# A walk of its own for each of 21 weight blocks: strided weights, regrouped columns, split matmuls

## The chip, the cores and the metric

The kernel runs on one core of a Trainium2 chip. The metric is the device time of one execution in microseconds, the median over the runs of the kernel. A second view is one profiled execution, whose span is counted from its first to its last instruction.

## The reference

One decoder block over 256 tokens of width 2048, in float32: an attention branch and a state-space branch, merged by gates, and then a feed-forward part. What the change touches is the up-projection of that last part:

```python
D_MODEL = 2048
SEQ = 256
D_FF = 5632
...
        x = x + merged @ w_out[i]
        h = rms_norm(x, ffn_norm_g[i])
        val, gate = jnp.split(h @ w_up[i], 2, axis=-1)
        gate = causal_depthwise_conv(gate, conv_w[i], conv_b[i])
        x = x + (val * jax.nn.gelu(gate, approximate=False)) @ w_down[i]
    return rms_norm(x, final_norm_g)
```

`w_up` is 2048 x 11264, by far the largest of the weights. The kernel holds the activations transposed, with the features on the 128 partitions and the 256 tokens along the columns.

## The kernel before

**Units and blocks.** Every weight matrix is cut into units of 128 partitions x 1024 columns (512 KB). A unit holds eight 128 x 128 weight tiles. 416 units are walked in one fixed order, `units`. The projections q, kv, u, ga, gs, the attention and state-space outputs A and S, glu and o come first. Then come the 22 up-projection blocks `up0` to `up21` of eight units each (block j yields 256 value and 256 gate features), and four down-projection blocks `dn0` to `dn3`.

**Precision.** The kernel keeps nearly full float32 precision with matmuls of a reduced format, `float32r`. ScalarE rounds a unit `raw` to `whi` (a CAST), and VectorE computes the rest, `wlo = raw - whi`. The activations are split likewise, once, into `Ah` and `Al`, which lie side by side in `x2g`: for each of the 16 groups of 128 features there are 256 columns of `Ah` and then 256 of `Al`. A product is then `whi*Ah + whi*Al + wlo*Ah`.

**Two ways to multiply.** In the first stages and in `up0` each weight tile takes three matmuls of 256 columns (`whi` with `Ah`, `whi` with `Al`, `wlo` with `Ah`), all into one accumulator. From `up1` on, and in `dn0` to `dn2`, the accumulator is a whole 512-column bank of PSUM for each tile. There one matmul of 512 columns takes `whi` over `Ah` and `Al` together, and one of 256 columns takes `wlo` over `Ah` into the first half. These two matmuls are called a **pair** below. A block has 16 feature groups x 4 tiles = 64 pairs. The two halves of the bank are added when the block is read out (`whole`, in `ev_up`). Each matmul instruction loads its own 128 x 128 weight tile first, also where it is the same tile as before.

**What sets the order.** The order is written out: the loop over the units multiplies unit i, and then `prep(i + LOOK)` rounds the unit five places ahead and issues the load of the unit nine places ahead (`load(i + 4)` inside `prep`). There are four buffers of `raw` and five each of `whi` and `wlo`. The program keeps clocks of its own, `clk_v`, `clk_a` and `clk_pe`, only to decide where the attention and state-space work is put in; that work is over before `up1`.

**Where the buffers lie.** A buffer of `whi` or `wlo` is a tile of 1032 floats, of which 1024 are used, so that the next buffer starts 4128 bytes on.

**The line numbers.** All engine calls go through the helper `Counted`, so almost every row of the profile has its one line, L132. Rows are told apart by the tile names.

Of the kernel before, what the change touches and what calls it, by code (L numbers as in the profile page):

```python
# [8 lines left out]
F32 = mybir.dt.float32  # L9
F32R = mybir.dt.float32r  # L10
I32 = mybir.dt.int32
AF = mybir.ActivationFunctionType
ALU = mybir.AluOpType
AX = mybir.AxisListType

P = 128
T = 256
# [6 lines left out]
LOOK = 5  # L24
# [33 lines left out]
def _units():  # L58
    def block(name, K, m):
        kw = 1024 // (m * P)  # L60
        return [(name, K, m, k0, kw) for k0 in range(0, K, kw)]

    def pair(x, y):
        return [u for both in zip(x, y) for u in both]

    out = pair(block("q0", NK, 4), block("u", NK, 4)) + block("kv", NK, 2) + block("q1", NK, 4)
    for n, K in (("ga", NK), ("gs", NK), ("A", 8)):
        for c in range(3 if n == "A" else 4):
            out += block(f"{n}{c}", K, 4)
    g0 = block("glu0", 4, 4)  # L70
    out += g0[:1] + block("A3x", 8, 2) + block("A3y", 8, 2) + g0[1:] + block("glu1", 4, 4) + pair(block("S0", 4, 4), block("S1", 4, 4))
    for n, c, K in [("S", 2, 4), ("S", 3, 4)] + [("o", c, NK) for c in range(4)]:
        out += block(f"{n}{c}", K, 4)
    for c in range(22):
        out += block(f"up{c}", NK, 4)
    for c in range(4):
        out += block(f"dn{c}", NFF, 4)
    return out


class Tally:
# [56 lines left out]
def hybrid_block_kernel(  # L138
# [14 lines left out]
    V, S = Counted(nc.vector, clk_v, dve_ns), Counted(nc.scalar, clk_a, act_ns)  # L153
    PE = Counted(nc.tensor, clk_pe, pe_ns)

    base = ctx.enter_context(tc.tile_pool(name="base", bufs=1))
    strm = ctx.enter_context(tc.tile_pool(name="strm", bufs=1))
# [6 lines left out]
    def close_pool(cm):  # L164
        cm.__exit__(None, None, None)
# [17 lines left out]
    A = base.tile([P, NK, 2, T], F32R, tag="A", name="xg")  # L183
# [21 lines left out]
    units = _units()  # L205
# [14 lines left out]
    def load(u, parts=1):  # L220
        if u >= NU:
            return
        raws[u] = strm.tile([P, 1024], F32, tag="raw", name=f"raw{u}", bufs=4)
        arrive[u] = fetch(1456.0, clk_v.ns if u > 3 else 0.0)
        n = 1024 // parts
        for i in range(parts):
            nc.sync.dma_start(raws[u][:, i * n : (i + 1) * n], wst[u, :, i * n : (i + 1) * n])

    prepped = {}

    def prep(i, parts=1):
        if i >= NU:
            return
        raw = raws.pop(i)
        clk_a.ns = max(clk_a.ns, clk_pe.ns if i >= LOOK else 0.0, arrive.pop(i))
        hi = strm.tile([P, 1032], F32R, tag="whi", name=f"whi{i}", bufs=LOOK)[:, 0:1024]
        lo = strm.tile([P, 1032], F32R, tag="wlo", name=f"wlo{i}", bufs=LOOK)[:, 0:1024]
        n = 1024 // parts
        for j in range(parts):
            sl = slice(j * n, (j + 1) * n)  # L240
            S.copy(hi[:, sl], raw[:, sl])
            clk_v.ns = max(clk_v.ns, clk_a.ns + 130.0)
            V.tensor_tensor(lo[:, sl], raw[:, sl], hi[:, sl].bitcast(F32), op=ALU.subtract)
        prepped[i] = (hi, lo, clk_v.ns)
        if i >= 4:
            load(i + 4)
# [51 lines left out]
    st = {}  # L298
# [514 lines left out]
    def finish(key):  # L813
        while key not in st:
            assert any([advance(e, True) for e in list(gens)])
# [146 lines left out]
    def begin(name):  # L962
        if name == "glu0":
            finish("su1")
        elif name == "o0":
            st["X"] = base.tile([P, NK, T], F32, tag="X", name="xres")
            nc.gpsimd.dma_start(st["X"], xT)
            A2 = base.tile([P, NK, 2, T], F32R, tag="A", name="x2g")
            st["A"], st["Ah"], st["Al"] = A2, A2[:, :, 0], A2[:, :, 1]
            A2 = mid.tile([P, 2, 4, T], F32, tag="tA", name="sqA")  # L970
            st["sq"], st["sq2"] = A2[:, 0], A2[:, 1]
        elif name == "dn0":
            A3 = base.tile([P, 2, NK, T], F32, tag="A", name="xo_sq")
            st["xo"] = A3[:, 0]
            st["sq"], st["sq2"] = A3[:, 1, 0:4], A3[:, 1, 4:8]
# [27 lines left out]
    def drain():  # L1003
        while held:
            after(clk_v, clk_pe)
            after(clk_a, clk_pe)
            evac(*held.pop(0))

    for i, (name, K, m, k0, kw) in enumerate(units):
        if k0 == 0:  # L1010
            begin(name)
            if name == "q1":
                finish("rs")
                drain()
            elif name == "A0":
                finish("attn")
            elif name == "o0":
                finish("m3")
            elif name == "up1":
                finish("rs2")  # L1020
                assert not gens and not aux
            if name[:2] == "dn" or name[:2] == "up" and name != "up0":
                if name == "up1":
                    close_pool(ax_cm)
                    wide_cm, pool = open_pool("wide_b", space=PSUM, side="right")
                    wide = [pool]
                elif name == "up2":
                    close_pool(acc_cm)
                    wide_cm2, pool = open_pool("wide_a", space=PSUM, side="left")
                    wide.append(pool)  # L1030
                nf += 1
                accs[name] = wide[nf % 2 - 1].tile([P, 4, 512], F32, tag="wide", name=f"acc_{name}")
            elif name == "kv":
                accs[name] = bank("pq", m, T)
            elif name[:2] == "A3":
                accs[name] = bank("at" if name == "A3x" else "pq", m, T)
            else:
                accs[name] = accp.tile([P, m, T], F32, tag="acc", name=f"acc_{name}")
        if name == "glu0" and k0 == 2:
            finish("su3")  # L1040
        acc = accs[name]
        mh, ml = mover(name)
        hi, lo, ready = prepped.pop(i)
        clk_pe.ns = max(clk_pe.ns, ready)
        hi = hi.rearrange("p (k m c) -> p k m c", k=kw, m=m)
        lo = lo.rearrange("p (k m c) -> p k m c", k=kw, m=m)
        if name == "dn3" and i >= NU - TAIL:
            tail.append((k0, hi, lo))
            prep(i + LOOK)
            continue  # L1050
        double = acc.shape[2] == 512 and name != "dn3"
        for kk in range(kw if double else 0):
            k = k0 + kk
            both = (st["A"] if name[0] == "u" else st["H"])[:, k].rearrange("p s t -> p (s t)")
            for c in range(m):
                PE.matmul(acc[:, c], hi[:, kk, c], both, start=k == 0, stop=False, skip_group_check=True)
                PE.matmul(acc[:, c, 0:T], lo[:, kk, c], mh[:, k], start=False, stop=k == K - 1, skip_group_check=True)
        for kk in range(0 if double else kw):
            k = k0 + kk
            for c in range(m):  # L1060
                o = acc[:, c, 0:T]
                first = k == 0 and (c % 2 == 0 or name == "dn3")
                last = k == K - 1
                PE.matmul(o, hi[:, kk, c], mh[:, k], start=first, stop=False, skip_group_check=True)
                PE.matmul(o, hi[:, kk, c], ml[:, k], start=False, stop=False, skip_group_check=True)
                PE.matmul(o, lo[:, kk, c], mh[:, k], start=False, stop=last, skip_group_check=True)
                run_aux()
            if kk == 0:
                fill()
        if i + LOOK < NK:  # L1070
            xg(i + LOOK, "ag")
        if i in (1, 3):
            load_x(i + 11, 2)
        if i == 3:
            nc.sync.dma_start(pr[:, 48:], par[:, 48:])
            nc.sync.dma_start(ident, cst[:, 0:P])
        if i == 6:
            nc.sync.dma_start(cs, cst[:, P:512])
            nc.sync.dma_start(cT, ssmc)
            st["consts"] = True  # L1080
        for e in gens:
            e[1] -= 1
        fill()
        if k0 + kw == K:
            held.append((name, acc))
        prep(i + LOOK)
        if "rs" in st:
            drain()
        if k0 + kw == K and name == "o3":
            spawn(g_norm2())  # L1090
        if k0 + kw == K and name == "dn2":
            spawn(g_pre(), 2)
# [17 lines left out]
    for n in range(4):  # L1110
        o = (aux, acc)[n % 2][:, n // 2 * 2, 0:T]
        for k0, hi, lo in tail:
            for kk in range(2):
                k = k0 + kk
# [20 lines left out]
    for c0, c1 in zip(cuts, cuts[1:]):  # L1135
        o = xo[:, c0:c1]
# [102 lines left out]
```

## Time and profile before

| what | value |
|---|---|
| median of 2 runs | 1249.06 us (1249.02 to 1249.1) |
| the profiled execution, its time | 1248.1 us |
| the profiled execution, its span | 1246.3 us |
| granted TensorE clock over the span | 0.996 |
| PE (matmuls) busy | 99% of the span, 8476 matmuls |
| PEld (weight loads) busy | 90%, 8476 loads |
| VectorE busy | 69% |
| ScalarE busy | 50% |
| DMA | 228.29 MB, mean 183 GB/s |

PE is the matrix engine and PEld its weight loads, which overlap the matmuls. Matmuls are pipelined, so that one shown with 280 ns can start 118 ns after the one ahead of it: the cost of a matmul in a stream is read from the distance of the starts, not from its duration. The chain of work that ended last is the list of the profile that says what the end of the kernel waited for, back to its first instruction. Shapes read as partitions x elements.

### The profile page before, as it was taken

Reading aid. Unit: us, or ns where it says so; the run is one execution under the profiler, and the core shown is the slowest. Engines: PE = TensorE matmul, PEld = TensorE weight load, DVE = VectorE, ACT = ScalarE, POOL = GpSimd, SP = SyncE. Lnnn points to the kernel's source line nnn. Section 1 sums busy time; section 2 is a strip of 40 time slices with the busy share of each in tenths; the row PEclk is TensorE's granted clock in tenths of the full one; section 3 lists DMA queues with packets and bytes.
Section 4 is the critical chain, followed back from the end, with each engine's and each line's share of the span. In section 5 each row is a group of like instructions: output and inputs, shape, how many; then the busy total and the mean of one; then the engine's idle time right before and its main releaser. Section 6 shows DMA issues by size and latency. Waiting matters only on the chain.

```text
span 1246.3 us, 20901 instructions
## 1 busy us (share of the span) xinstructions
PE 1232.6 (99%) x8476; PEld 1127.8 (90%) x8476; DVE 857.5 (69%) x1220; ACT 619.8 (50%) x865; POOL 10.4 (1%) x24
## 2 busy tenths in 40 slices
PE   9999999999999999999999999999999999999996
PEld 9999999899999999988888888888888888888996
DVE  6987888889978656666767666666676654454543
ACT  7667455454435545544555445455455444343531
POOL 0000000000000000000000000000000000000000
PEclk9999999999999999999999999999999999999998
DMA  8655444444445665555564655646546564656451
GB/s 313 208 196 185 154 151 159 144 160 155 155 169 184 240 197 175 178 192 171 179 219 144 218 186 172 216 153 212 194 151 219 171 221 160 218 162 218 156 201 68
DMA packets 64896, 228.29 MB, mean 183 GB/s; under 512 B 7648, under 2 KB 9056, under 8 KB 64672
## 3 DMA queue, kind: packets, MB, share of 16 engines
q1 hardware_dynamic: 63648, 223.55, 54.1%
q0 software_dynamic: 1152, 3.41, 0.9%
q8 instruction: 66, 1.08, 0.4%
q14 instruction: 30, 0.25, 0.1%
HBM read 224.31 MB, written 2.10 MB: 182 GB/s over the span
## 4 chain that ended last, share of the span: by engine, by line
PE 97%; DVE 1%; DMA 0%; ACT 0%; SPq 0%; issue 0%; DVEq 0%
PE acc_up L132 40%; PE acc_dn L132 19%; PE acc_ga L132 8%; PE acc_gs L132 7%; PE acc_o L132 7%; PE acc_q L132 3%; PE acc_A L132 3%; PE pq L132 2%; PE at L132 2%; PE acc_S L132 2%; PE acc_u L132 1%; PE yp L132 1%; PE acc_glu L132 1%; PE aux L132 1%; DVE xo_sq L132 0%; DMA x_in<-in_xT_dram 0%
## 5 line engine op out<-in xcount | busy, mean ns | idle before, releaser
L132 DVE TENSOR_TENSOR wlo<-raw,whi 128x1024 fp32r<-128x1024 f32 (+2 forms) x421 | 501.5, 1210 | 272.4 <-ACT whi L132 268.4
L132 ACT CAST whi<-raw 128x1024 fp32r<-128x1024 f32 (+2 forms) x421 | 428.9, 1037 | 416.0 <-PE acc_dn L132 110.4
L132 PE MATMUL acc_up<-x2g,whi 128*128 128x512 f32 (+1 forms) x1472 | 494.1, 385 | 0.0
L132 PE MATMUL acc_up<-x2g,wlo 128*128 128x256 f32 x1408 | 395.1, 281 | 0.0
L132 PEld LDWEIGHTS acc_up<-x2g,whi 128*128 128x128 f32 x1472 | 272.1, 188 | 59.0
L132 PEld LDWEIGHTS acc_up<-x2g,wlo 128*128 128x128 f32 x1408 | 265.3, 188 | 0.0
L132 PE MATMUL acc_dn<-H,whi 128*128 128x512 f32 (+1 forms) x856 | 242.7, 351 | 0.0
L132 PE MATMUL acc_dn<-H,wlo 128*128 128x256 f32 x692 | 194.0, 280 | 0.0
L132 PEld LDWEIGHTS acc_dn<-H,whi 128*128 128x128 f32 x856 | 149.2, 188 | 22.8
L132 PEld LDWEIGHTS acc_dn<-H,wlo 128*128 128x128 f32 x692 | 130.7, 189 | 0.0
L132 PE MATMUL acc_ga<-xg,whi 128*128 128x256 f32 x512 | 93.4, 284 | 0.0
L132 PE MATMUL acc_gs<-xg,whi 128*128 128x256 f32 x512 | 93.2, 284 | 0.0
L132 PEld LDWEIGHTS acc_ga<-xg,whi 128*128 128x128 f32 x512 | 78.4, 188 | 2.8 <-issue 2.0
L132 PEld LDWEIGHTS acc_gs<-xg,whi 128*128 128x128 f32 x512 | 78.3, 188 | 2.6 <-issue 1.7
L132 PE MATMUL acc_ga<-xg,wlo 128*128 128x256 f32 x256 | 72.0, 281 | 0.0
L132 PE MATMUL acc_gs<-xg,wlo 128*128 128x256 f32 x256 | 72.0, 281 | 0.0
L132 PE MATMUL acc_o<-mh,whi 128*128 128x256 f32 x256 | 71.8, 281 | 0.0
L132 PE MATMUL acc_o<-ml,whi 128*128 128x256 f32 x256 | 71.7, 280 | 0.0
L132 PE MATMUL acc_o<-mh,wlo 128*128 128x256 f32 x256 | 71.6, 280 | 0.0
L132 ACT ACTIVATE cy<-cy 128x512 f32<-128x512 f32 x22 | 13.9, 632 | 69.9 <-DVE cy L132 69.9
L132 PEld LDWEIGHTS acc_o<-mh,wlo 128*128 128x128 f32 x256 | 48.2, 188 | 0.0
L132 PEld LDWEIGHTS acc_ga<-xg,wlo 128*128 128x128 f32 x256 | 48.2, 188 | 0.0
(212 smaller groups left out, 1407.8 us busy)
## 6 DMA issues: line engine op xcount, KB each, us to landing
raw<-in_wst_dram SPq DMA_DIRECT2D x415, 512.0 KB, 4.3
xres<-in_xT_dram POOLq DMA_DIRECT2D x1, 2048.0 KB, 10.1
x_in<-in_xT_dram SPq DMA_DIRECT2D x7, 256.0 KB, 5.8
out_dram<-xo_sq SPq DMA_DIRECT2D x7, 256.0 KB, 2.4
br<-in_ssmb_dram POOLq DMA_DIRECT2D x3, 256.0 KB, 4.9
raw<-in_wst_dram SPq DMA_DIRECT2D x2, 256.0 KB, 2.9
cT<-in_ssmc_dram SPq DMA_DIRECT2D x1, 512.0 KB, 5.1
us<-ul POOLq DMA_DIRECT2D x16, 32.0 KB, 2.6
```

The lines of the kernel that those rows point to most:

```text
L132: return fn(*a, **k)
```

## The change

The change touches the blocks `up1` to `up21` and the place of all the weight buffers. Each of the 21 blocks gets a triple `(ws, g, one)` of the table `FORMS`, in order:

- `ws` is the **weight step**. For `ws` 1 a tile's 128 columns are neighbours, as before. For 2, 4 or 8, that many tiles are interleaved, so that a tile's next column is 2, 4 or 8 floats (8, 16 or 32 bytes) on. The CAST and the subtraction write `whi` and `wlo` in that order (`woven`), the subtraction reads `whi` in that order, and the matmul loads its weights with that step (`wt`).
- `g` is the **column walk**. For 0 the moving columns go in order, as before. For g of 4 to 32 the matmul takes every second group of g columns first and then the groups between; the output columns go the same way (`mv`). For -1 both go backwards.
- `one` is 1 for one matmul of 512 columns with `whi`, as before, and 0 for two of 256, each with its own weight load.

The first block's triple `(1, 0, 1)` is the walk of before. Seven blocks have step 2 (`up8` to `up14`), four step 4 (`up15` to `up18`) and one step 8 (`up21`). Ten blocks are split (`one` = 0): `up5` to `up7`, `up11` to `up14`, `up17`, `up18` and `up20`. Twelve are walked in groups: g = 4 in `up2`, 8 in `up12`, 16 in six and 32 in four. `up19` and `up20` go backwards. The results are the same sums, in the same places of PSUM.

The buffers of all 416 units become tiles of 1040 floats, and the used part starts 0, 4, 8, 12 or 12 floats into its tile, by the unit's number modulo 5.

```diff
+FORMS = [(1, 0, 1), (1, 4, 1), (1, 16, 1), (1, 32, 1), (1, 0, 0), (1, 16, 0), (1, 32, 0),
+         (2, 0, 1), (2, 16, 1), (2, 32, 1), (2, 0, 0), (2, 8, 0), (2, 16, 0), (2, 32, 0),
+         (4, 0, 1), (4, 16, 1), (4, 0, 0), (4, 16, 0), (1, -1, 1), (1, -1, 0), (8, 0, 1)]
...
+    def woven(i, ap, rows=False):
+        name = units[i][0]
+        s = FORMS[int(name[2:]) - 1][0] if name[:2] == "up" and name != "up0" else 1
+        if s == 1:
+            return ap
+        if rows:
+            return ap.rearrange("p (a s c) -> p a s c", s=s, c=P)
+        return ap.rearrange("p (a c s) -> p a s c", c=P, s=s)
...
-        hi = strm.tile([P, 1032], F32R, tag="whi", name=f"whi{i}", bufs=LOOK)[:, 0:1024]
-        lo = strm.tile([P, 1032], F32R, tag="wlo", name=f"wlo{i}", bufs=LOOK)[:, 0:1024]
+        o = (0, 4, 8, 12, 12)[i % LOOK]
+        hi = strm.tile([P, 1040], F32R, tag="whi", name=f"whi{i}", bufs=LOOK)[:, o : o + 1024]
+        o = (0, 4, 8, 12, 12)[i % LOOK]
+        lo = strm.tile([P, 1040], F32R, tag="wlo", name=f"wlo{i}", bufs=LOOK)[:, o : o + 1024]
...
-            S.copy(hi[:, sl], raw[:, sl])
+            S.copy(woven(i, hi[:, sl]), woven(i, raw[:, sl], True))
...
-            V.tensor_tensor(lo[:, sl], raw[:, sl], hi[:, sl].bitcast(F32), op=ALU.subtract)
+            V.tensor_tensor(woven(i, lo[:, sl]), woven(i, raw[:, sl], True), woven(i, hi[:, sl].bitcast(F32)),
+                            op=ALU.subtract)
...
-        for kk in range(kw if double else 0):
+        form = FORMS[int(name[2:]) - 1] if double and name[:2] == "up" else None
+        if form:
+            ws, g, one = form
+
+            def mv(ap):
+                return ap[:, ::-1] if g < 0 else ap.rearrange("p (n t g) -> p t n g", t=2, g=g) if g else ap
+
+            def wt(w, b):
+                w = w.rearrange("p k m c -> p (k m c)")
+                if ws < 2:
+                    return w[:, P * b : P * b + P]
+                return w.rearrange("p (a c s) -> p a c s", c=P, s=ws)[:, b // ws, :, b % ws]
+
+            for kk in range(kw):
+                k = k0 + kk
+                xb = st["A"][:, k].rearrange("p s t -> p (s t)")
+                for c in range(m):
+                    for o in (slice(0, 2 * T),) if one else (slice(0, T), slice(T, 2 * T)):
+                        PE.matmul(mv(acc[:, c, o]), wt(hi, kk * m + c), mv(xb[:, o]), start=k == 0 and o.start == 0,
+                                  stop=False, skip_group_check=True)
+                    PE.matmul(mv(acc[:, c, 0:T]), wt(lo, kk * m + c), mv(xb[:, 0:T]), start=False, stop=k == K - 1,
+                              skip_group_check=True)
+        for kk in range(kw if double and not form else 0):
```

No instruction changes its place on any engine. What changes is the form of matmuls, CASTs and subtractions, and that a split block has 64 matmuls more. On PE, the start of block `up2`, form `(1, 4, 1)`; before:

```order
L132 MATMUL acc_up_6542<-x2g,whi_6424 128x512
L132 MATMUL acc_up_6542<-x2g,wlo_6425 128x256
L132 MATMUL acc_up_6542<-x2g,whi_6424 128x512
L132 MATMUL acc_up_6542<-x2g,wlo_6425 128x256
L132 MATMUL acc_up_6542<-x2g,whi_6424 128x512
```

And now (the helper's line is L139 after the change; the last number is g, and the one ahead of it the groups of each of the two rounds):

```order
L139 MATMUL acc_up_6542<-x2g,whi_6424 128x2x64x4
L139 MATMUL acc_up_6542<-x2g,wlo_6425 128x2x32x4
L139 MATMUL acc_up_6542<-x2g,whi_6424 128x2x64x4
L139 MATMUL acc_up_6542<-x2g,wlo_6425 128x2x32x4
L139 MATMUL acc_up_6542<-x2g,whi_6424 128x2x64x4
```

The same pairs stand in the same places; only their columns are taken in two rounds. On PE, the start of block `up17`, form `(4, 0, 0)`; before:

```order
L132 MATMUL acc_up_9497<-x2g,whi_9383 128x512
L132 MATMUL acc_up_9497<-x2g,wlo_9384 128x256
L132 MATMUL acc_up_9497<-x2g,whi_9383 128x512
L132 MATMUL acc_up_9497<-x2g,wlo_9384 128x256
L132 MATMUL acc_up_9497<-x2g,whi_9383 128x512
```

And now:

```order
L139 MATMUL acc_up_9945<-x2g,whi_9831 128x256 x2
L139 MATMUL acc_up_9945<-x2g,wlo_9832 128x256
L139 MATMUL acc_up_9945<-x2g,whi_9831 128x256 x2
L139 MATMUL acc_up_9945<-x2g,wlo_9832 128x256
L139 MATMUL acc_up_9945<-x2g,whi_9831 128x256 x2
```

Each matmul of 512 columns has become two of 256, so that a pair is now three matmuls with three weight loads; the step of the weights does not show in these rows.

## The prediction

> **What bounds the kernel now.** I read the chain of work that ended last first, for what the end of the kernel waits for. The page has it by engine and line:
>
> ```profile
> PE 97%; DVE 1%; DMA 0%; ACT 0%; SPq 0%; issue 0%; DVEq 0%
> ```
>
> So only what happens to the matmul stream counts at first order. The same chain in order of time, for the stages o, `up` and `dn` (start us, us, what, count):
>
> ```profile
> 400.59 90.36 PE acc_o L132 x768
> ...
> 506.35 479.28 PE acc_up L132 x2757
> 985.63 238.13 PE acc_dn L132 x1512
> ```
>
> These rows give the price of a matmul in an unbroken stream. Stage o has matmuls of 256 columns alone: 90.36 / 768 = 117.7 ns each. The `up` row holds 69 more of that kind, from the end of `up0` (8.12 us), and then 21 x 128 = 2688 matmuls, that is 21 blocks or 1344 pairs, in 471.16 us. So a block is **22.44 us** and a pair **350.6 ns**, of which the 512-column matmul takes 350.6 - 117.7 = 232.9.
>
> Next I read the timeline inside a block, matmuls and weight loads together (start us, us):
>
> ```profile
> 700.14 0.40 PE L132 MATMUL acc_up<-x2g,whi 128*128 128x512 f32 x1
> 700.15 0.19 PEld L132 LDWEIGHTS acc_up<-x2g,wlo 128*128 128x128 f32 x1
> 700.38 0.28 PE L132 MATMUL acc_up<-x2g,wlo 128*128 128x256 f32 x1
> 700.38 0.19 PEld L132 LDWEIGHTS acc_up<-x2g,whi 128*128 128x128 f32 x1
> 700.49 0.39 PE L132 MATMUL acc_up<-x2g,whi 128*128 128x512 f32 x1
> ```
>
> A load starts when the matmul ahead of its own starts, and not earlier. One load is under way per matmul. The load from 700.38 ends at 700.57, and its matmul starts at 700.49, 0.08 us before that end. So a load of length L keeps two matmul starts at least L - 80 ns apart: 188 - 80 = 108 ns today, just inside the 117.7 of 256 columns. **The weight load is the second bound of the stream**, covered with 10 ns to spare by 256 columns, and with 125 by 512.
>
> What a load costs by its columns (last column: mean ns):
>
> ```profile
> L132 PEld LDWEIGHTS acc_up<-x2g,wlo 128*128 128x128 f32 x1408 | 265.3, 188 | 0.0
> ...
> L132 PEld LDWEIGHTS yp<-xa,cT 128*32 128x32 f32 x64 | 5.7, 109 | 5.5
> ...
> L132 PEld LDWEIGHTS at<-pt,vtok 128*64 128x64 f32 x64 | 3.9, 136 | 2.2
> ```
>
> From 64 to 128 columns it grows by 52 ns, from 32 to 64 by 27: 0.82 ns per column, so 105 of the 188 ns go with the columns.
>
> **The change part by part.** *Split matmuls.* Where loads stay as they are, three matmuls of 117.7 take the place of 350.6: 353.1, or +2.5 x 64 = 0.16 us a block. Eight of the ten split blocks have steps 1 or 2: 1.3 us.
>
> *Weight step.* No load with a step is in the trace. The nearest rows are VectorE's reads when it fills the table E by doubling. The rows with 64 elements read runs of 2 floats out of every 512 bytes, those with 32 single floats, those with 128 and 256 runs of 4 and 8:
>
> ```profile
> L132 DVE TENSOR_TENSOR ea<-E 128x256 f32<-128x256 f32 x1 | 0.4, 425 | 0.0
> ...
> L132 DVE TENSOR_TENSOR ea<-E 128x128 f32<-128x128 f32 x1 | 0.3, 294 | 0.0
> ...
> L132 DVE TENSOR_TENSOR ea<-E 128x64 f32<-128x64 f32 x1 | 0.2, 235 | 0.0
> L132 DVE TENSOR_TENSOR ea<-E 128x32 f32<-128x32 f32 x1 | 0.2, 233 | 0.0
> ```
>
> The slope from 128 to 256 is 1.02 ns per element. On that line 64 elements should take 229 (measured 235) and 32 should take 196 (measured 233). Runs of two are nearly free, and a single float per place costs 37 / 32 = 1.2 ns more, about double. The same in another row, 16 single floats against 16 neighbours:
>
> ```profile
> L132 DVE TENSOR_TENSOR sp<-E x3: 190/192/194, 108.4 to 108.9; 128x16 f32<-128x16 f32 x3
> ...
> L132 DVE TENSOR_TENSOR sp<-sp 128x16 f32<-128x16 f32 x7 | 0.9, 171 | 0.0
> ```
>
> 21 / 16 = 1.3 ns more. I carry this over to the loads: step 2 free, steps 4 and 8 double the 105 ns. The Trainium skill, SBUF — State Buffer, section Specifications (TRN2), gives lines of 16 bytes that need at least two hits each for full bandwidth; two floats a line remain with step 2, one with 4 or 8. For VectorE the rows agree; no row here shows it for a weight load, and the sums stand on the rows alone.
>
> A doubled load is 293 ns. Starts are then 293 - 80 = 213 ns apart, or 117.7 + 105 = 223 if the load sets the 117.7 already; I take 218. A whole pair (`up15`, `up16`, `up21`): the 512-column matmul still covers its load, so 232.9 + 218 = 451, +100.3 x 64 = 6.4 us a block, **19.3 us**. A split pair (`up17`, `up18`): 3 x 218 = 654, +303.4 x 64 = 19.4 us a block, **38.8 us**. The bounds: nothing, where a load reads each float at one price whatever the step; a gain is excluded, since 117.7 is then set by the columns. And 1.3 x 128 = 168 ns more a load, by the dearest row: starts 276 to 286 apart, say 281; whole pairs +211 (13.5 us x 3), split ones +492 (31.5 us x 2), 103.5 us together. I take the doubling, as it is the row with the most elements.
>
> *CAST and subtraction.* They are off the chain while they keep up. In one block (us, busy per engine):
>
> ```profile
> 520.00:542.43 22.43, 22.43 (x131) 19.61 (x130) 12.58 (x14) 11.40 (x14) 0.00 (x0) 1.00 0.58 187
> ```
>
> The columns after the length are PE, PEld, VectorE and ScalarE. Steps 4 and 8 make eight subtractions of a block read single floats: 8 x 1024 x 1.2 = 9.8 us, VectorE 22.4. That fills a block of today, but such a block lasts 28.9 us or more in the sum; if its loads stay short, the lead of five units (11 us and more) takes up what is over. ScalarE has 11.40 and no strided row; doubled writes would add 8 x 1.05 = 8.4, also covered. Both cost nothing.
>
> *Column walk.* Groups of 4 to 32 keep runs of at least four floats, which cost VectorE nothing in the rows above. I take 0 here and for backwards; it is rival D.
>
> *Buffer places.* They reach all 416 units. Three units in a row, each from its first matmul to the next one's:
>
> ```profile
> 632.13:634.97 2.84, 2.84 (x19) 1.00 0.27 107
> 634.97:637.74 2.77, 2.77 (x19) 1.00 0.00 0
> 637.74:640.55 2.81, 2.81 (x19) 1.00 0.00 0
> ```
>
> The same matmuls take 2.84 and 2.77 us at a granted clock of 1.00. The second and third units pass without a byte of DMA (0.00), so it isn't the loads; the buffers differ. Against the mean, 22.44 / 8 = 2.805, that is ±0.035 us: ±14.6 us over 416 units if all fell on one side. I take 0, since the old places were mixed and the new ones are too.
>
> **The sum:** 1.3 + 19.3 + 38.8 = +59.4 us. The profiled execution took 1248.1 (span 1246.3, the rest before and behind it), so 1307.5. The median of the runs is 1.0 above that execution: **1308 us**.
>
> **The rivals.** *B, the loads don't care for the step.* The order of the weights then changes nothing on PE, ten splits cost 1.6 us, and it ends at 1251, within 2%. For it: loads run on a path of their own, and VectorE's price need not hold there. It decides up to a load of 198 ns (117.7 + 80), beyond which 256 columns no longer cover it; the doubled load has 293. The Trainium skill, TensorE: Matmul & The Clock Gate, section LDWEIGHTS (loading the stationary operand), has a load's time go by its columns alone, P / 1.2 ns: by that rule it is B, 1251. The three rows above agree, but all have dense weights.
>
> *C, step 2 costs too,* half as much as 4: starts 168 ns apart in seven blocks, 3.2 us in each of three whole ones and 9.8 in each of four split ones, some 48 on top: 1357. Against it: 235 measured where 229 is on the line.
>
> *D, the walk breaks the stream.* If each jump between groups cost 1.1 ns, about what a single place costs VectorE, a pair has 768 / g jumps: 13.5 us for `up2`, 6.8 for `up12`, 3.4 in four blocks with g = 16 (two more hide behind slow loads) and 1.7 in four with 32. That is 41 us on top: 1349; backwards blocks would come under it too. For it: no matmul of the trace has such columns. The Trainium skill, PSUM — Partial Sum Buffer, section Specifications (TRN2), says that any non-contiguous access slows matmuls significantly; its lines there are of 8 bytes, which runs of four floats fill. No run here shows it yet.
>
> *E, faster.* The new places and walks win the whole spread of 2.84 to 2.77 for all units: 416 x 0.07 = 29 us, 1220, and the loads cost nothing. Against it: it needs B, and a mixed set of places as good as the best.
>
> **How the numbers follow.** The forecast has 0.56, B 0.18, D 0.13, C 0.08, E 0.05. A kernel 2% off, 25 us, can be told from no change. The forecast's own range is 1291 (placement, the 213) to 1354 (the dear load). The range of 8 in 10 takes in B with most of its placement, D and half of C: 1240 to 1360. It leaves out E and the outer ends of the others, below 2 in 10. Slower by over 2%: forecast, C and D, less a little for partly covered loads, 0.75. Within: B and that little, 0.20. Faster: E, 0.05.
>
> **What would show it.** Block lengths in the chain or the windows: 22.4 us for `up1`, the same for `up2` to `up4` and `up8` to `up10`, 22.6 for split blocks of steps 1 and 2, 28.9 for `up15`, `up16` and `up21`, 41.9 for `up17` and `up18`. Weight loads of 293 ns in those five blocks and 188 in all others. Subtractions of 2.4 us there, and no PE idle time ahead of these blocks. Stage o at 117.7 ns a matmul within 1%. It is wrong if loads of step 4 stay at 188 (B), if those of step 2 grow (C), if `up2` is longer than `up4` (D), or if block `up1`, whose walk is the old one, moves by more than 1% (placement).

## The result: 1324.87 us, 6% slower

The changed kernel takes 1324.87 us (median of 2 runs, 1324.72 to 1325.02) against 1249.06 before: a ratio of 1.0607, with a 95% interval of 1.0561 to 1.0653. The prediction was 1308 us, with a range of 1240 to 1360. The profiled execution has a span of 1323.0 us at a granted clock of 0.997 (before: 1246.3 us at 0.996), so the clock has no part in it.

The page of the changed kernel: busy time by engine, and the chain of work that ended last by engine.

```profile
PE 1308.7 (99%) x9116; PEld 1239.7 (94%) x9116; DVE 892.1 (67%) x1220; ACT 666.0 (50%) x865; POOL 10.4 (1%) x24
...
PE 98%; DVE 1%; DMA 0%; ACT 0%; SPq 0%; issue 0%; DVEq 0%
```

The matmul stream still sets the end, with 640 matmuls more than the 8476 of before (ten split blocks x 64). The same chain in order of time (start us, us, what, count):

```profile
400.75 90.89 PE acc_o L139 x768
...
507.01 555.15 PE acc_up L139 x3397
1062.15 238.28 PE acc_dn L139 x1512
```

The `up` stage alone has grown, from 479.28 to 555.15 us: +75.9 of the 76.7 by which the span grew. Stage o grew by 0.5, dn by 0.15, and the start of the `up` row moved by 0.7.

Next, single blocks in the table of windows: from the first matmul of a block to the first of the next, for `up1`, `up2`, `up3`, `up5`, `up8`, `up11`, `up15`, `up17` and `up21`. The columns are length, then busy time of PE, PEld, VectorE, ScalarE and GpSimd, granted clock, DMA share, GB/s.

```profile
514.93:537.29 22.36, 22.36 (x131) 19.63 (x129) 14.06 (x16) 11.73 (x13) 0.00 (x0) 1.00 0.61 187
537.29:559.67 22.38, 22.38 (x131) 19.61 (x129) 15.09 (x18) 11.29 (x14) 0.00 (x0) 1.00 0.53 169
559.67:582.65 22.98, 22.98 (x130) 19.70 (x129) 15.36 (x19) 11.30 (x14) 0.00 (x0) 1.00 0.58 183
605.51:628.11 22.60, 22.60 (x194) 22.60 (x193) 15.23 (x19) 11.30 (x14) 0.00 (x0) 1.00 0.53 184
674.26:696.72 22.46, 22.46 (x131) 20.10 (x129) 14.83 (x18) 11.92 (x14) 0.00 (x0) 1.00 0.57 183
742.62:765.59 22.97, 22.97 (x194) 22.97 (x193) 15.15 (x18) 12.02 (x14) 0.00 (x0) 1.00 0.53 181
835.00:865.01 30.01, 30.01 (x130) 30.01 (x129) 23.30 (x20) 18.92 (x14) 0.00 (x0) 1.00 0.54 166
895.28:940.36 45.08, 45.08 (x195) 45.08 (x193) 22.51 (x19) 19.48 (x15) 0.00 (x0) 1.00 0.33 97
1030.84:1061.99 31.15, 31.15 (x130) 31.15 (x129) 21.96 (x20) 16.02 (x15) 0.00 (x0) 1.00 0.53 167
```

Block `up1`, whose walk is the old one, takes 22.36 us (22.43 on average before). The three whole blocks of steps 4 and 8 take 30.01, 30.26 (`up16`) and 31.15; the two split ones 45.08 and 45.16 (`up18`). These five make +69.5 us, the other sixteen +6.5. In the five, PEld is busy for the whole length. That alone does not make a block slow: in the split blocks `up5` and `up11` it is busy throughout as well. The timeline inside `up15` shows more (start us, us; four loads, three matmuls):

```profile
850.38 0.31 PEld L139 LDWEIGHTS acc_up<-x2g,whi 128*128 128x128 f32 x1
850.49 0.51 PE L139 MATMUL acc_up<-x2g,whi 128*128 128x512 f32 x1
850.59 0.33 PEld L139 LDWEIGHTS acc_up<-x2g,wlo 128*128 128x128 f32 x1
850.84 0.28 PE L139 MATMUL acc_up<-x2g,wlo 128*128 128x256 f32 x1
850.85 0.31 PEld L139 LDWEIGHTS acc_up<-x2g,whi 128*128 128x128 f32 x1
850.96 0.51 PE L139 MATMUL acc_up<-x2g,whi 128*128 128x512 f32 x1
851.06 0.33 PEld L139 LDWEIGHTS acc_up<-x2g,wlo 128*128 128x128 f32 x1
```

From `whi` load to `whi` load it is 0.47 us; before, it was 0.35. The records of the two loads overlap by about 0.1 us, so a load's price is read from the distance of the starts, as with matmuls: 0.21 and 0.26 us here, 235 ns on average. The 512-column matmul takes 231 in an unbroken stream, so both matmuls of the pair now go at the pace of the loads (2 x 235 = 470; the block gives 30.01 / 64 = 469 ns a pair). Loads grouped by tile, in `up15` and then in `up8` (last columns: busy us, mean ns, idle before):

```profile
L139 PEld LDWEIGHTS acc_up<-x2g,wlo 128*128 128x128 f32 x62 | 20.6, 331 | 0.0
L139 PEld LDWEIGHTS acc_up<-x2g,whi 128*128 128x128 f32 x63 | 19.5, 310 | 0.0
...
L139 PEld LDWEIGHTS acc_up<-x2g,whi 128*128 128x128 f32 x61 | 11.9, 195 | 2.2
L139 PEld LDWEIGHTS acc_up<-x2g,wlo 128*128 128x128 f32 x60 | 11.8, 196 | 0.0
```

A load of step 4 shows 310 to 331 ns, one of step 2 195, and one of step 1 188 before.

### The profile page after: what moved, and what is told of

Same layout as the page of the kernel before. It is cut to its first block, busy times and chain, and to the rows that moved or that the text cites. A ratio compares the mean times of both kernels' runs of the same rounds, so it can differ in the third digit from the quotient of the medians.

```text
span 1323.0 us, 22181 instructions
## 1 busy us (share of the span) xinstructions
PE 1308.7 (99%) x9116; PEld 1239.7 (94%) x9116; DVE 892.1 (67%) x1220; ACT 666.0 (50%) x865; POOL 10.4 (1%) x24
## 4 chain that ended last, share of the span: by engine, by line
PE 98%; DVE 1%; DMA 0%; ACT 0%; SPq 0%; issue 0%; DVEq 0%
PE acc_up L139 43%; PE acc_dn L139 18%; PE acc_ga L139 7%; PE acc_gs L139 7%; PE acc_o L139 7%; PE acc_q L139 3%; PE acc_A L139 3%; PE pq L139 2%; PE at L139 2%; PE acc_u L139 2%; PE acc_S L139 2%; PE yp L139 1%; PE acc_glu L139 1%; PE aux L139 1%; DMA raw<-in_wst_dram 0%; DVE xo_sq L139 0%
## 5 line engine op out<-in xcount | busy, mean ns | idle before, releaser
L139 DVE TENSOR_TENSOR wlo<-raw,whi 128x1024 fp32r<-128x1024 f32 (+2 forms) x421 | 536.2, 1292 | 315.0 <-ACT whi L139 312.2
L139 ACT CAST whi<-raw 128x1024 fp32r<-128x1024 f32 (+2 forms) x421 | 475.6, 1153 | 443.4 <-PE acc_dn L139 110.5
L139 PE MATMUL acc_up<-x2g,whi 128*128 128x256 f32 (+1 forms) x2112 | 560.9, 346 | 0.0
L139 PEld LDWEIGHTS acc_up<-x2g,whi 128*128 128x128 f32 x2112 | 410.5, 220 | 22.7
L139 PE MATMUL acc_up<-x2g,wlo 128*128 128x256 f32 x1408 | 413.2, 293 | 0.0
L139 PEld LDWEIGHTS acc_up<-x2g,wlo 128*128 128x128 f32 x1408 | 315.7, 224 | 0.0
L139 PE MATMUL acc_dn<-H,whi 128*128 128x512 f32 (+1 forms) x856 | 242.8, 351 | 0.0
L139 PE MATMUL acc_dn<-H,wlo 128*128 128x256 f32 x692 | 194.0, 280 | 0.0
L139 PEld LDWEIGHTS acc_dn<-H,whi 128*128 128x128 f32 x856 | 149.5, 188 | 22.9
L139 PEld LDWEIGHTS acc_dn<-H,wlo 128*128 128x128 f32 x692 | 130.5, 189 | 0.0
L139 PE MATMUL acc_ga<-xg,whi 128*128 128x256 f32 x512 | 93.2, 285 | 0.0
L139 PE MATMUL acc_gs<-xg,whi 128*128 128x256 f32 x512 | 93.1, 284 | 0.0
L139 PEld LDWEIGHTS acc_ga<-xg,whi 128*128 128x128 f32 x512 | 78.2, 189 | 2.8 <-issue 2.0
L139 PEld LDWEIGHTS acc_gs<-xg,whi 128*128 128x128 f32 x512 | 78.2, 189 | 2.6 <-issue 1.7
L139 PE MATMUL acc_o<-mh,whi 128*128 128x256 f32 x256 | 72.0, 281 | 0.0
L139 PE MATMUL acc_o<-mh,wlo 128*128 128x256 f32 x256 | 72.0, 281 | 0.0
L139 PE MATMUL acc_o<-ml,whi 128*128 128x256 f32 x256 | 72.0, 281 | 0.0
L139 PE MATMUL acc_gs<-xg,wlo 128*128 128x256 f32 x256 | 71.8, 280 | 0.0
L139 PE MATMUL acc_ga<-xg,wlo 128*128 128x256 f32 x256 | 71.7, 280 | 0.0
L139 ACT ACTIVATE cy<-gb,pr 128x256 f32<-128x256 f32 x44 | 24.1, 594 | 51.5 <-DVE gb L139 51.5
L139 ACT ACTIVATE cy<-cy 128x512 f32<-128x512 f32 x22 | 13.9, 632 | 69.9 <-DVE cy L139 69.9
L139 PEld LDWEIGHTS acc_o<-mh,whi 128*128 128x128 f32 x256 | 48.3, 189 | 0.0
```

The lines of the kernel that those rows point to most:

```text
L139: return fn(*a, **k)
```

## The experiments

The trace gave the place and the size, but two parts of the change meet in the five blocks: the stepped load on PE and the stepped writing on ScalarE and VectorE. The theory was that the loads alone do it; the rival, that the writing side has a share. Four kernels of one chip tell them apart.

**No steps.** All weight steps become 1; column walks, splits and buffer places stay.

```diff
-        s = FORMS[int(name[2:]) - 1][0] if name[:2] == "up" and name != "up0" else 1
+        s = 1
...
-            ws, g, one = form
+            ws, g, one = 1, form[1], form[2]
```

> All weight steps set to 1 in storage and in the loads; column walks, splits and buffer places stay. Theory L (a weight load with a step of 4 or 8 floats takes about 235 ns in place of at most 117 and sets the distance of matmuls): blocks up15 to up18 and up21 fall from 30.0, 30.3, 45.1, 45.2 and 31.2 us to 22.4 to 23.1, loads are 188 ns everywhere, about 1255 us in all. Rival W (the CAST and the subtraction in steps hold PE up): the same 1255, since they are undone as well; the two next kernels tell L from W. Rival F (the splits, column walks and places cost most of it): 1300 or more.

Measured: 1255.18 us (1254.86 to 1255.61), a ratio of 1.0054 (1.0038 to 1.0069) to before. The chain's row of the stage, and the two around it:

```profile
400.10 90.89 PE acc_o L139 x768
...
506.36 485.84 PE acc_up L139 x3397
992.20 238.26 PE acc_dn L139 x1512
```

The row is 69.3 us shorter than with the steps. `up15` is back at 22.34, `up17` at 22.60, `up21` at 22.38. The steps make 69.3 us. The 6.6 us that stay above the 479.28 of before are splits, walks and places together.

**Loads in steps, written densely.** The CAST and the subtraction write as before; only the matmuls load with a step. The tiles' columns are mixed by it, which leaves the amount of work as it is.

```diff
-        s = FORMS[int(name[2:]) - 1][0] if name[:2] == "up" and name != "up0" else 1
+        s = 1
```

> The reverse: stored in order, loaded with the steps of the change (again a mixture of tiles, not the reference's result). Theory L: 1322 to 1326 us, block up17 45 us, loads 310 to 330 ns. Rival W: about 1255.

Measured: 1324.22 us (one run). Its chain row:

```profile
506.32 555.15 PE acc_up L139 x3397
```

That is the 555.15 us of the full change to the hundredth, and the 21 block lengths agree with the full change within 0.01 us. The stepped loads alone make the 69.3 us.

**Written in steps, loaded densely.** The other half, with the tiles mixed likewise.

```diff
-            ws, g, one = form
+            ws, g, one = 1, form[1], form[2]
```

> CAST and subtraction write with the steps as in the change, but the loads read 128 neighbouring floats, so that a matmul gets a mixture of tiles (the result is not the reference's). Theory L: about 1255 us, loads 188 ns, block up17 22.6 us, though subtractions of 2.0 us and CASTs of 2.0 us remain. Rival W: about 1325, with PE idle ahead of the step-4 blocks.

Measured: 1279.02 us (one run), where 1255 was expected: a miss of 24 us. Most matmul starts are as quick as without steps, 232 and 118 ns, but the five blocks take 24.83, 28.46, 27.06, 27.46 and 28.70 us. Busy time in `up1` and in two stretches of the step-4 blocks (columns as above):

```profile
514.93:537.29 22.36, 22.36 (x131) 19.61 (x130) 14.06 (x16) 11.72 (x13) 0.00 (x0) 1.00 0.59 187
833.00:859.80 26.80, 24.91 (x144) 21.34 (x143) 21.76 (x19) 18.89 (x15) 0.00 (x0) 1.00 0.51 155
859.80:888.00 28.20, 24.76 (x131) 20.84 (x130) 22.91 (x19) 20.02 (x15) 0.00 (x0) 0.94 0.52 165
```

PE now stands idle for 1.9 and 3.4 us, and the granted clock of the second stretch is 0.94. In all, the five blocks are 23.0 us longer than without steps. PE is idle for 13.3 us of them. The other 9.7 us pass with PE busy, nearly all of them in `up16`, `up17`, `up18` and `up21`, where the granted clock is 0.94, 0.94, 0.94 and 0.88 (0.69 from 876 to 880 us, where the longest idle time ends; 1.00 in `up19` and `up20`, which have no idle time). The waits of these four blocks, 830 to 945 us (engine and tile that waited, for whom; us in total, times, longest):

```profile
PEld acc_up L139 <- DVE wlo L139: 7.2, 4, 1.8
...
PE acc_up L139 <- DVE wlo L139: 6.1, 4, 1.5
PEld acc_up L139 <- ACT whi L139: 5.0, 4, 2.2
PE acc_up L139 <- ACT whi L139: 3.9, 4, 1.9
```

And the two operations behind them there (mean ns after the busy time):

```profile
L139 ACT CAST whi<-raw 128x1024 fp32r<-128x1024 f32 x35 | 64.3, 1933 | 8.2 <-DMA raw<-in_wst_dram 6.7 <-DVE wlo L139 1.3
...
L139 DVE TENSOR_TENSOR wlo<-raw,whi 128x1024 fp32r<-128x1024 f32 x36 | 67.7, 1935 | 11.8 <-ACT whi L139 11.1 <-PE acc_up L139 0.6
```

Both take 1.93 us; with dense writing, in `up1` to `up4`, the CAST takes 1.05 and the subtraction 1.22. VectorE then has 20 to 23.5 us of work in each of the five blocks, which PE could do in 22.3 to 23.1, and ScalarE has 15 to 20. At the end of a block both also read it out, in a chain of operations that wait for one another. In one such place the last subtraction ends at 865.1 us, the next CAST starts at 873.2, and PE stands idle up to 875.3 and again up to 877.3. So the stepped writing is not free: it costs 23.8 us (1279.02 - 1255.18) where the loads are quick, the lower clock behind the idle times included. In the full change the slow loads make the blocks 30 to 45 us long, and that cover hides all of it, as the row of 555.15 without it shows.

**Buffer places alone.** The kernel before, with the new tiles of 1040 floats and the starts 0, 4, 8, 12, 12.

```diff
-        hi = strm.tile([P, 1032], F32R, tag="whi", name=f"whi{i}", bufs=LOOK)[:, 0:1024]
+        o = (0, 4, 8, 12, 12)[i % LOOK]
+        hi = strm.tile([P, 1040], F32R, tag="whi", name=f"whi{i}", bufs=LOOK)[:, o : o + 1024]
```

> The kernel before with the new buffer places alone (1040 floats, start 0 to 12 floats in). If places cost nothing: 1249 us within 1. If they carry the 6.5 us that the sixteen quick blocks lost: 1255; if the old places were the worse ones, as a single block could suggest (22.36 in place of 22.43): 1247.

Measured: 1246.48 us (1246.18 to 1248.85, 11 runs) against 1248.64 on the same chip, a ratio of 0.9988 (0.9979 to 0.9997). That is 0.1% under the kernel before, which matters to nobody. The 21 blocks take 469.8 us against 471.1, most of them 22.29 to 22.36 us each; so the other parts of the change are best read against 22.36.

**No splits.** All ten split blocks become whole; steps, walks and places stay.

```diff
-            ws, g, one = form
+            ws, g, one = form[0], form[1], 1
```

> The change with one matmul of 512 columns in all 21 blocks; steps, walks and places stay. If a stepped load costs its 235 ns for each matmul, the split blocks up17 and up18 fall from 45.1 and 45.2 us to 30.0 and 30.3, and the eight other split ones lose 0.1 to 0.5 us each: 1293 us. If the load cost a step-4 block the same however often it is loaded, 1320 or more.

Measured: 1292.69 us (1292.48 to 1293.02), ratio 1.0351 (1.0334 to 1.0368), as expected. The splits cost 32.2 us of the 75.8, and 30.0 of these by the third stepped load of each pair in `up17` and `up18` (45.08 - 30.00 and 45.16 - 30.24).

**What sets the load's price: steps and columns.** The next kernel uses the 21 blocks as a test bench. Each form is a step, a number of weight columns, a number n of moving columns and a number of repeats; the products don't add up to the reference's.

```diff
+            every, wide_w, n, reps = form
...
+                    for r in range(reps):
+                        for w in (hi, lo):
+                            PE.matmul(acc[0:wide_w, c, 0:n], wt(w, b), xb[:, 0:n], start=False,
+                                      stop=k == K - 1 and r == reps - 1 and w is lo, skip_group_check=True)
```

> Measures the load by itself. Each of the blocks up1 to up21 takes another weight step (1, 2, 3, 4, 5, 6, 8 floats), weight width (128, 64, 32 columns) and matmul length (64, 256, 512 columns), always whi and wlo in turn, some of them repeated so that PE stays the bound; the sums aren't the reference's. Read: the median distance of matmul starts in the last seven units of a block. Theory L with lines of 16 bytes at 1.83 ns a line (235 / 128): for 64 columns 107 to 118 ns at steps 1 and 2, 176 at step 3, 235 at 4, 5 and 6, 241 at 8. Rival, a price that grows with the distance: 3 near 176, but 5 and 6 clearly above 4. At 256 columns 118, 120, 235, 241 for steps 1, 2, 4, 8; at 512 columns 233, 233, 235, 241, since the columns cover the load. Width 64 at step 1: about 60 for 64 columns; at 256 columns 118 if the columns set it, 109 or less if the load sets it.

Measured, as the median distance of matmul starts in each block, in ns (weights of 128 columns unless said):

| step | n = 64 | n = 256 | n = 512 |
|---|---|---|---|
| 1 | 213 | 118 | 231 |
| 2 | 213 | 120 | 233 |
| 3 | 213 | - | - |
| 4 | 235 | 235 | 236 |
| 5 / 6 | 222 / 223 | - | - |
| 8 | 238 | 241 | 246 |
| 1, 64 columns | 58 | 117 | 230 |
| 4, 64 columns | 119 | - | - |
| 1, 32 columns | - | 114 | 231 |

The load of step 4 takes 235 ns whatever moves beside it, and half as long for half the columns. The column of n = 64 had a surprise: 107 to 118 ns were expected there for steps 1 and 2, and 176 for step 3. Windows in the blocks of step 1 and of step 4 with n = 64, and of step 4 with n = 512:

```profile
530.00:600.00 70.00, 70.00 (x330) 70.00 (x329) 6.13 (x5) 5.22 (x5) 0.00 (x0) 0.50 0.12 38
...
843.00:902.00 59.00, 59.00 (x252) 58.73 (x250) 14.90 (x18) 10.04 (x12) 0.00 (x0) 0.50 0.23 72
...
1275.00:1300.00 25.00, 25.00 (x107) 25.00 (x107) 12.04 (x15) 9.75 (x12) 0.00 (x0) 1.00 0.45 143
```

The granted clock is 0.50 in the first two. There the dense load takes 213 ns (70 us / 329), while the one of step 4 takes 235 (59 / 250 = 236) at half the clock as at the full one (25 / 107 = 234). So the price of step 4 is not one in cycles of TensorE. (The load of 64 columns with step 4 had a clock of 0.54, the dense one of 64 columns 1.00.)

**What sets it: lines.** That pointed to the reading of SBUF. The theory: each line of 16 bytes, four floats, that a load or a moving matrix touches takes its reader about 1.8 ns, however much of it is used; a dense load touches 32 lines, step 2 64, steps 4 and above 128. The rival: a price for any step from 4 on. The test bench again, with step 3, with moving columns of which runs start on or across a line, and with bf16, which has eight numbers in a line.

```diff
+            kind, a, n, reps = form
...
+                s, o = a if kind == "load" else 1, 4 * (b % 2)
+                return w[:, o : o + (P - 1) * s + 1 : s]
...
+                if kind == "bf":
+                    return st["bf"][:, 0 : (n - 1) * a + 1 : a]
+                if kind == "run":
+                    off, g = a
+                    return xb[:, off : off + n].rearrange("p (n t g) -> p t n g", t=2, g=g)
```

> Asks whether one rule holds for both streams of PE: a line of 16 bytes of SBUF costs about 1.8 ns, whoever reads it (512 float32r columns are 128 lines, 231 ns; a load of step 4 is 128 lines, 235 ns). Blocks differ in loads (steps 1 to 7 at 128 to 512 columns), in runs of columns that lie on the lines or across them (start shifted by 2 floats), and in operands of bfloat16, half as many lines; the sums aren't the reference's. Line theory, median distances in ns: step 3 176 (96 lines), steps 5 to 7 222 to 241 (128 lines), step 4 at 512 columns 236. 256 columns in runs of 4: 117 on the lines, 230 across them (128 lines); in runs of 8: 118 and 173 (96 lines). bfloat16: 256 columns 107 to 110, 512 columns 214 to 217, which the clock then sets; every second element of 256, as many lines as float32r, 116; every fourth of 128, 116. Rival (a share of each stream is lost whatever is read): bfloat16 118 and 231, runs across lines 117 to 120.

Measured (one run; medians; of some 4950 matmuls three have no record):

| what | lines read | ns | ns per line |
|---|---|---|---|
| load, step 1 (n = 128 to 192) | 32 | 112 | - |
| load, step 2 | 64 | 118 | 1.84 |
| load, step 3 | 96 | 175 | 1.82 |
| load, step 4 | 128 | 235 | 1.84 |
| load, steps 5 / 6 / 7 | 128 | 225 / 227 / 234 | 1.76 to 1.83 |
| moving 256, runs of 4 on a line | 64 | 118 | 1.84 |
| the same, 2 floats on, across lines | 128 | 229 | 1.79 |
| moving 256, runs of 8 on lines | 64 | 118 | 1.84 |
| the same, 2 floats on | 96 | 170 | 1.77 |
| bf16, moving 256 / 512 | 32 / 64 | 109 / 216 | - |
| bf16, every second of 256 | 64 | 113 | 1.77 |
| bf16, every fourth of 128 | 64 | 116 | 1.81 |

Two stretches by tile: loads of step 3 (two blocks, 698 to 786 us), and the matmuls with runs of four across lines (941 to 995 us). Their records overlap (262 ns long here, 331 at step 4), so count and time are what to read:

```profile
L141 PEld LDWEIGHTS acc_up<-x2g,whi 128*128 128x128 f32 x255 | 66.2, 261 | 0.0
L141 PEld LDWEIGHTS acc_up<-x2g,wlo 128*128 128x128 f32 x249 | 65.4, 263 | 0.0
...
L141 PE MATMUL acc_up<-x2g,whi 128*128 128x256 f32 x118 | 48.4, 410 | 0.0
L141 PE MATMUL acc_up<-x2g,wlo 128*128 128x256 f32 x118 | 48.4, 410 | 0.0
```

88 us / 504 loads is 175 ns, and 54 / 236 is 229. Step 3 lies halfway between 2 and 4, where the rival had no price for it, and the same 256 columns cost 118 or 229 by where they start. A line costs 1.76 to 1.84 ns in all ten rows that have the figure, with loads and moving columns alike. The two readers don't add up: a step-4 load (235) beside 512 columns (231) takes 235. Below a floor the line is not what counts: a dense load takes 112 and 256 bf16 columns 109, though both touch only 32 lines. The two stepped bf16 rows are weak evidence for that reason. The 113 ns lies only 4 above the 109 of dense columns, and in the row of 116 the loads run back to back at 116 ns each, so that they may set it. The Trainium skill, SBUF — State Buffer, section Specifications (TRN2), gives lines of 16 bytes that need at least two hits each for full bandwidth. For loads the runs nearly agree: step 2, with two floats of each line, takes 118 ns against 112. For moving float32r columns they do not: two floats of a line at a time double the matmul, as the next run shows.

**The column walk.** The same bench for the walks, on the reading side (in), the writing side (out) or both, with dense loads. This run was planned beside the one of loads, before the theory of lines.

```diff
+            g, side = form
...
+                return ap.rearrange("p (n t g) -> p t n g" if side in on else "p (t n g) -> p t n g", t=2, g=g)
...
+                        PE.matmul(mv(acc[:, c, o], ("both", "out")), w[:, kk, c], mv(xb[:, o], ("both", "in")),
```

> Measures the column walk by itself: steps 1, pairs of 512 and 256 columns; blocks differ in the group size g (1 to 128 columns) and in which side is walked in groups: the columns read, those written, or both (with one side alone the sums land in other places than the reference's). Rival D of the forecast (a price per jump): the block grows as g falls, 1.1 ns a jump would be 13.5 us at g = 4 and 27 at 2. Theory B (only some distances hurt, such as 64 and 128 bytes): 22.4 us at g = 2, 4 and 8, 22.9 to 23.0 at 16 and 32. If it is the read, the blocks with the read side alone show it and those with the written side alone stay at 22.4; if the write, the reverse.

Measured, block lengths in us (no walk: 22.36; g = 1, in: 43.61; g = 128, both: 22.39):

| g | both | in | out |
|---|---|---|---|
| 2 | 43.54 | 43.54 | 22.37 |
| 4 | 22.38 | 22.49 | 22.37 |
| 8 | 22.43 | 22.42 | 22.35 |
| 16 | 22.95 | 23.06 | 22.34 |
| 32 | 22.88 | 22.86 | 22.35 |
| 64 | 22.36 | 22.29 | 22.35 |

Windows of g = 2 in, g = 2 out and g = 16 in:

```profile
646.95:690.49 43.54, 43.54 (x130) 26.53 (x128) 15.54 (x18) 11.47 (x15) 0.00 (x0) 1.00 0.30 97
690.49:712.86 22.37, 22.37 (x129) 19.62 (x128) 14.78 (x18) 11.29 (x14) 0.00 (x0) 1.00 0.43 142
870.25:893.31 23.06, 23.06 (x131) 19.68 (x129) 15.49 (x19) 11.29 (x14) 0.00 (x0) 1.00 0.55 184
```

The writing side costs nothing at any g from 2 on. On the reading side half a line at a time doubles the matmuls (451 and 229 ns). Neither theory of the expectation had that (22.4 us, or 27 more); it is what lines say, since each is read twice. Groups of 16 and 32 cost 0.5 to 0.7 us a block, nearly all in the 512-column matmul (up to 240 ns instead of 231), those of 4, 8 and 64 nothing or 0.1. Neither lines nor a price per jump gives that order, and its cause stays open.

## Why the prediction was right, and where it was off

- **The stream as the only path, and a load that becomes its bound:** right. The chain is 98% PE, and the run with the loads alone has the same 555.15 us.
- **Starts L - 80 ns apart:** it holds for dense loads and drifts with the step. A load's record is longer than the distance of starts by 80 ns for dense loads (192 and 112, in the run on lines), 79 with step 2 (197 and 118), 87 with step 3 (262 and 175) and 97 in the split block `up17` of step 4 (332 and 235). The wait behind it reads otherwise there: a load starts 0.10 us behind the matmul ahead of its own, not with it, and its own matmul starts 0.19 us before the load's recorded end, not 0.08. What was too short is the doubled load, 293 instead of 332. Here two errors ran against each other: 332 - 80 would have given 252.
- **The size of the doubled load:** this is the term that failed. I took 218 ns between starts, from VectorE's rows; it is 235. That is 128 lines at 1.84 ns, which no dense row could show. The price of VectorE's single floats is not what sets a load, so that 218 came as near as it did is partly luck. A whole pair takes 469 ns instead of 451: 17 of the 18 ns are the longer load of the 256-column matmul. The other load is no longer covered either, since 235 is over the 231 of 512 columns, but that adds only 1 or 2 ns. The whole blocks cost +24.1 us (predicted 19.3), the split ones +45.4 (38.8). That is 11.4 of the 16.4 us by which +59.4 fell short of +75.8.
- **Eight other split blocks, 1.3 us, and the walk, 0:** too low, since these blocks and the other whole ones together show +6.5. The run without steps lets them be added up, against the 22.36 of the new places. The reading walk with g = 16 and 32 costs 0.4 to 0.7 us in each of eight blocks, 4.2 together. A split costs 0.24 (`up5`: 22.60), not 0.16, so 1.9. The steps of 2 make 1.1, and walking backwards makes 0.4 (`up19` 22.60; no run looks into its cause). The places win about 1.2 back. The rows of VectorE on which I put the walk at 0 don't speak for TensorE's reader.
- **Step 2 free:** nearly. Its load is 195 instead of 188 ns, 118 between starts instead of 112, and `up8` takes 0.1 us more than `up1`. In a split block, where every load faces 256 columns, it shows more: `up11` takes 22.97 us, and 22.62 without steps. Rival C, 3.2 us in a whole block and 9.8 in a split one, falls.
- **CAST and subtraction cost nothing:** right for this change, wrong in one reason. The subtraction takes 2.05 us in the blocks of step 4 (predicted 2.4), the CAST 2.08. The slow loads cover both. But I had claimed that the lead of five units takes up what is over if the loads stay short; the run with dense loads paid 23.8 us for it. VectorE's 20 to 23.5 us of work fill a block of 22.4, so I take it that the lead which the read-out uses up is not won back; no run measures the lead itself.
- **Buffer places, 0 within 14.6:** right; -0.1%.
- **The rivals:** B (loads that don't care, 1251) is what the run without steps shows, 1255, but not the change. The rule behind it, the Trainium skill's TensorE: Matmul & The Clock Gate, section LDWEIGHTS (loading the stationary operand), by which columns alone set a load's time, fails here: 112, 118, 175 and 235 ns at 128 columns with steps 1, 2, 3 and 4. D falls by `up2`, 22.38, with the most jumps. Beside D I put a rule of the Trainium skill, PSUM — Partial Sum Buffer, section Specifications (TRN2), by which any non-contiguous access slows matmuls significantly. On the written side it is not borne out from groups of two floats on (22.37 against 22.36). E falls with the loads.

## What to carry to other kernels

Lay stationary weights so that a tile's columns are neighbours, or at most every second float: the reader pays per line of four floats, 1.8 ns here. From step 4 on that doubles a load (235 ns instead of 112); a 256-column matmul (118) no longer covers it, and one of 512 (231) not quite. Before a load is called hidden, add up the loads of a whole pair against its matmuls (470 against 351 here), since the shorter matmul shows the gap first. And an engine that is off the chain only because the chain is slow comes back when the chain is mended: price it against the quick version too.

## What was not expected of the hardware

- A line of 16 bytes takes 1.76 to 1.84 ns to read, in loads and in moving columns of float32r, and the two readers run side by side (the bf16 rows fit, but hardly test it). It also fits that 512 columns of float32r take 231 ns: they are 128 lines. The 216 ns of 512 bf16 columns are not set by their 64 lines, which would take 115.
- In a stream of matmuls with 64 columns and dense full loads the granted clock is 0.50 and a load takes 213 ns; with 128 to 192 columns the clock is 1.00 and the load takes 112. With 64 moving columns and weights of 64 columns the clock is 1.00 too, and a load takes 58, so it is not the short matmul alone. What decides stays open.
- Steps 5 and 6 are cheaper than 4 (222 to 227 against 235), and 8 is dearer (238 to 246), though all touch 128 lines. That stays open, as does the 0.5 to 0.7 us of the reading walk with groups of 16 and 32.
